# The fourth token form of the Strassen feed-forward moved to another place modulo 512 bytes in SBUF, and the softmax statistics given pools of their own

## The chip, the cores and the metric

One NeuronCore of a Trainium2 chip, one launch. The metric is the device time of the program in microseconds, the median of the runs shown. Engines are named as in the profile: PE is the matrix engine (PEld its weight loads), DVE the vector engine, ACT the scalar engine, POOL the general engine, SP the queue that issues most DMAs.

## The reference

Two decoder layers on 512 tokens of width 1024. Each layer is a SwiGLU feed-forward block, a token mixer, and a second feed-forward block, each with a residual sum and a layer norm behind it. The first layer mixes by latent attention (12 heads) and the second by three-branch sparse attention (12 heads), both with 4 heads more that attend to a memory of 256 rows. All is float32.

```python
def swiglu(x, w_gu, w_down):                 # w_gu 1024 x 5632, w_down 2816 x 1024
    g, u = jnp.split(x @ w_gu, 2, axis=-1)
    return (jax.nn.silu(g) * u) @ w_down

x = layer_norm(DN_ALPHA * x + 0.5 * swiglu(x, ffn_w_gu[layer, 0], ffn_w_down[layer, 0]), ...)
```

The four feed-forward blocks are the larger part of the time and the part that the change is about.

## The kernel before, in words

**Operands in two parts.** Every float32 operand is split into a rounded high part and the rest (`split`, L198 on ACT and L199 on DVE), and a product is three matmuls: high times high, high times low, low times high. Weights come in units of 128 x 1024 float32 by DMA (`load`), and `prep` splits each into the tiles `whi` and `wlo`, which lie in two rings (`wring`, 3 buffers, and `W.extra`, 4 buffers). `unit` and `ahead` prepare units up to four ahead of the matmuls.

**A feed-forward block** (`ffn`) has 22 slices of 128 hidden features, in five groups of 4 or 5 (`GROUPS`). Per group it first computes the hidden features and then multiplies them with the down weights (`by_units`, `prod`, L404 to L409: 512 columns a matmul). A slice is computed in one of two ways. An "s" slice is a plain product (`single`, `feature_major`, L356 to L361). A "d" slice (`seven`) is Strassen's scheme: seven products of quarter size in place of eight. Only the first group of a block has "s" slices, two or three of them; all other 77 slices are sevens.

**A seven** makes seven calls of `quarter`, each of 12 matmuls that accumulate 256 columns into half a PSUM bank: four each at L369 and L370 (weights `whi`, moving operand high and low in turn), then four at L373 (weights `wlo`, moving operand high). In order, the moving operands are a quarter of the activations (`F.xhi`, `F.xlo`), another quarter, then token form 4, form 1, form 2, form 3, and a last quarter of the activations. The forms (`F.t`, tiles `t1h` to `t4l`) are sums and differences of quarters of the activations; `token_forms` makes them once per block or takes those of the block before.

```python
            ks = slice(off + k * P, off + (k + 1) * P)
            nc.tensor.matmul(ps, lhsT=hi[:, ks], rhs=xh[:, k], start=k == 0, stop=False)
            nc.tensor.matmul(ps, lhsT=hi[:, ks], rhs=xl[:, k], start=False, stop=False)
```

**Where things lie.** Pools are laid one behind the other from the left end of SBUF, `small` and the pools of a stage from the right. Nearly all tiles are multiples of 512 bytes, so a small tile at the head of a pool sets where all that follows lies modulo 512. In the built program `wraw`, `whi`, `wlo`, the hidden features `hhi` and `hlo`, and the tiles of both attention stages lie at 256 modulo 512. The tile "offset" of 448 bytes at the head of the pool `xp` puts the activations `xhi` and `xlo`, and the pool `fm` with all token forms behind them, at 192: 64 bytes below the weights. The memory operands `mhi` and `mlo` are put at 320, 64 bytes above. The small statistics of the softmax heads (negated maximum `nm`, reciprocal sum `rs`, three buffers each) are taken from `small` by `stat`.

**What sets the order.** Nothing is scheduled by a planner: each engine runs its instructions in the order written, with semaphore waits that the framework derives from tiles, and waits on what lay before at the same addresses.

Of the kernel before, what the change touches and what calls it, by code (L numbers as in the profile page):

```python
# [9 lines left out]
F32 = mybir.dt.float32  # L10
# [7 lines left out]
P = 128  # L18
T = 512
D = 1024  # L20
NT = 4
# [82 lines left out]
def tile_trunk(ctx: ExitStack, tc, a: dict, out):  # L104
# [6 lines left out]
    small = ctx.enter_context(tc.tile_pool(name="small", bufs=1, side="right", reuse_waits="tile"))  # L111
# [123 lines left out]
        i %= 8  # L235
        return (PS.left if i < 5 else PS.right).tile([P, 512], F32, tag=f"b{i}", name="bank")

    small.tile([P, 88], F32, name="rest")

    def stat(tag, bufs):  # L240

        return small.tile([P, 2, 4], F32, tag=tag, name=tag, bufs=bufs)

    def stile():
        return PS.left.tile([P, 512], F32, tag="s", name="s", bufs=3)
# [4 lines left out]
    def s2tile():  # L250
        return PS.left.tile([P, 1024], F32, tag="s2", name="s2", bufs=2)

    def s1tile():
        return PS.left.tile([P, 512], F32, tag="s1", name="s1")
# [7 lines left out]
    def open_f(scope):  # L262
        F.st = ExitStack()
        W.extra = F.st.enter_context(tc.tile_pool(name=f"wx{scope}", bufs=NEXTRA, reuse_waits="tile"))
        F.xp = F.st.enter_context(tc.tile_pool(name=f"xp{scope}", bufs=1, reuse_waits="tile"))
        F.xp.tile([P, 112], F32, name="offset")
        F.sm = F.st.enter_context(tc.tile_pool(name=f"sm{scope}", bufs=2, reuse_waits="tile"))
        F.x = [F.xp.tile([P, D], F32, name=f"x{t}") for t in range(NT)]
        F.bk = 0
        W.scope = scope  # L270
        W.count = 0
        F.fst = ExitStack()
        F.fm = F.fst.enter_context(tc.tile_pool(name=f"fm{scope}", bufs=1, reuse_waits="tile"))

    def close_f():
        F.st.close()
        W.scope = None
        W.extra = None
        W.early = 0

    def right_pool(name, bufs=1):
        st = ExitStack()
        pool = st.enter_context(tc.tile_pool(name=name, bufs=bufs, side="right", reuse_waits="tile"))
        return st, pool
# [58 lines left out]
    def mm3(ps, ahi, alo, bhi, blo, first, last):  # L343
        nc.tensor.matmul(ps, lhsT=ahi, rhs=bhi, start=first, stop=False)
        nc.tensor.matmul(ps, lhsT=ahi, rhs=blo, start=False, stop=False)
        nc.tensor.matmul(ps, lhsT=alo, rhs=bhi, start=False, stop=last)  # L346
# [431 lines left out]

    def mla_heads(cT):
        st = ExitStack()  # L780
        hp = st.enter_context(tc.tile_pool(name="mh", bufs=1, reuse_waits="tile"))
        F.pt = hp
        va = hp.tile([P, NT, 768], F32, name="va")
# [59 lines left out]
            yield  # L843

        def head(u):
            nm, rs = stat("nm", 3)[:, 0, :], stat("rs", 3)[:, 0, :]
            pp = hp.tile([P, 1280], F32, tag="p", name="pp", bufs=5)
            pbuf[u] = pp
            pr, par = divmod(u, 2)
            qt = qts.pop(u)  # L850
            k = kx[par][pr % 2]
            for i in (3, 2, 1, 0):
                s = stile()
                q = slice(i * P, (i + 1) * P)
                n = (i + 1) * P
                nk = max(n, 256)
                po = pp[:, P_OFF[i]:P_OFF[i] + n]
                mm3(s[:, :nk], qt[:, 0, q], qt[:, 1, q], k[:, 0, :nk], k[:, 1, :nk], True, False)
                nc.tensor.matmul(s[:, i * P:n], lhsT=identb, rhs=maskb, start=False, stop=True)
                nc.vector.tensor_reduce(nm[:, i:i + 1], s[:, :n], axis=AX.X, op=ALU.max, negate=True)  # L860
                nc.scalar.activation(po, s[:, :n], AF.Exp, bias=nm[:, i:i + 1], accum_out=rs[:, i:i + 1])
                if i in (2, 0):
                    nc.vector.tensor_scalar(rs[:, i:i + 2], rs[:, i:i + 2], 1e-30, None, op0=ALU.max)
                    nc.vector.reciprocal(rs[:, i:i + 2], rs[:, i:i + 2])
                    for t in (i, i + 1):
                        po = pp[:, P_OFF[t]:P_OFF[t] + (t + 1) * P]
                        nc.gpsimd.tensor_tensor(po, po, rs[:, t:t + 1].to_broadcast([P, (t + 1) * P]), op=ALU.mult)
                yield
# [16 lines left out]
        def scores():  # L885
            yield from memory_scores(lambda n: stile())
            for u in range(HEADS):
                yield from head(u)
# [212 lines left out]

    def nsa_heads(gt, qf):
        st = ExitStack()
        hp = st.enter_context(tc.tile_pool(name="nh", bufs=1, reuse_waits="tile"))
        F.pt = hp
        F.qx.append([hp.tile([P, 2, T], F32R, name=f"q{e}") for e in ("e", "o")])
# [14 lines left out]
        def weigh(rs, gi):  # L1121

            nc.vector.scalar_tensor_tensor(rs, rs, 1e-30, gi, op0=ALU.max, op1=ALU.mult)
            nc.vector.reciprocal(rs, rs)

        def head(u):
            nm, rs = (stat(e, 3).rearrange("p a (b r) -> p (a b) r", r=2) for e in ("nm", "rs"))
            pp = hp.tile([P, 2560], F32, tag="p", name="pp", bufs=5)
            pbuf[u] = pp
            pr, par = divmod(u, 2)  # L1130
            h = pr + 6 * par
            qt = F.qx[pr % 2][par]
            kt = (S.ke, S.ko)[par]
            for i in (3, 2, 1, 0):
                s = s1tile() if i == 1 else s2tile()
                q = slice(i * P, (i + 1) * P)
                n = (i + 1) * P
                for c0 in range(0, 2 * n, 512):
                    c1 = min(c0 + 512, 2 * n)
                    for x in range(2):  # L1140
                        nc.tensor.matmul(s[:, c0:c1], lhsT=qt[:, x, q], rhs=kt[:, x, c0:c1],  # L1141
                                         start=x == 0, stop=x == 1 and c1 < 2 * n)
                nc.tensor.matmul(s[:, 2 * n - 256:2 * n], lhsT=identb, rhs=maskb[:, None, :].to_broadcast([P, 2, P]), start=False, stop=True)
                sv = s[:, 0:2 * n].rearrange("p (b r k) -> p r b k", r=2, k=P)
                po = pp[:, 2 * P_OFF[i]:2 * P_OFF[i] + 2 * n].rearrange("p (r b k) -> p r b k", r=2, k=P)
                nc.vector.tensor_reduce(nm[:, i], sv, axis=AX.XY, op=ALU.max, negate=True)
                for r in range(2):
                    nc.scalar.activation(po[:, r], sv[:, r], AF.Exp,
                                         bias=nm[:, i, r:r + 1], accum_out=rs[:, i, r:r + 1])
                if i in (2, 0):  # L1150
                    weigh(rs[:, i // 2 * 2:i // 2 * 2 + 2], gt[:, i // 2 * 2:i // 2 * 2 + 2, 3 * h + 1:3 * h + 3])
                    for ii in (i // 2 * 2, i // 2 * 2 + 1):
                        n = (ii + 1) * P
                        po = pp[:, 2 * P_OFF[ii]:2 * P_OFF[ii] + 2 * n].rearrange("p (r k) -> p r k", r=2)
                        nc.gpsimd.tensor_tensor(po, po, rs[:, ii, :, None].to_broadcast([P, 2, n]), op=ALU.mult)
                yield
# [24 lines left out]
        def scores():  # L1181
            for u in range(HEADS):
                yield from head(u)
# [50 lines left out]
    for side in ("left", "right"):  # L1234
        psum_pool(side, "f0")
    open_f(0)
    new_xt()
    new_blocks()
    sst, sp = right_pool("x0")
# [34 lines left out]
    for side in ("left", "right"):  # L1274
        psum_pool(side, "h0")
    mla_heads(cT)
    psum_pool("right", "f1")
    ast.close()
    shared_pool()
    open_f(1)  # L1280
    out_proj(0)
    mst.close()
# [14 lines left out]
    for side in ("left", "right"):  # L1297
        psum_pool(side, "h1")
    nsa_heads(gt, qf)
    psum_pool("right", "f2")  # L1300
    ast.close()
    S.st.close()
    open_f(2)
    out_proj(1)
    mst.close()
# [154 lines left out]
```

## Time and profile before

| what | value |
|---|---|
| median of 3 runs | 1894.77 us (1894.02 to 1897.25) |
| the profiled execution's own time | 1892.34 us |
| its span, from the first to the last instruction | 1890.1 us |
| PE busy | 1861.7 us, 98% |
| PEld busy | 1669.1 us, 88% |
| DVE busy | 1469.8 us, 78% |
| ACT busy | 869.5 us, 46% |
| granted TensorE clock, mean of the span | 0.997 |

The profile is of one execution. A matmul's row gives its start and a modelled end, and matmuls overlap: the time from one start to the next, here called the pace, is what a matmul costs in a stream, not its duration. Times in rows count from the first instruction.

### The profile page before, as it was taken

How to read it: one execution, taken by the hardware profiler on the slowest of the kernel's cores; microseconds unless marked ns; L12 is line 12 of the kernel's file. 1: busy time of each engine (PE TensorE's matmuls, PEld its weight loads, DVE VectorE, ACT ScalarE, POOL GpSimd, SP SyncE). 2: the span in 40 equal slices, each digit the busy share in tenths (PEclk: the TensorE clock that was granted, in tenths of full speed). 3: DMA queues.
4: the chain of work that ended last, by engine and by line, in shares of the span. 5: the costliest groups of instructions: out<-in, count | busy, mean ns of one | idle time of the engine just before them, and what ended most of it. 6: DMA issues, size and time to landing. Idle time of an engine off the chain costs nothing.

```text
span 1890.1 us, 31915 instructions
## 1 busy us (share of the span) xinstructions
PE 1861.7 (98%) x12776; PEld 1669.1 (88%) x12776; DVE 1469.8 (78%) x2362; ACT 869.5 (46%) x1435; POOL 164.2 (9%) x185
## 2 busy tenths in 40 slices
PE   9999999999999999999999999999999999999998
PEld 8999999886679999999999999998956689999997
DVE  7798788757658789788887987987577478887887
ACT  5344345446545335334663433444466344434432
POOL 0000000025500000000100000001255200000000
PEclk9999999999999999999999999999999999999999
DMA  6333335530133234234333323334321224323322
GB/s 237 112 112 109 115 101 153 171 106 27 64 112 133 80 101 134 79 101 146 115 128 113 123 79 101 123 110 158 107 50 28 94 82 138 107 83 112 114 82 74
DMA packets 59700, 203.85 MB, mean 108 GB/s; under 512 B 6944, under 2 KB 7216, under 8 KB 59552
## 3 DMA queue, kind: packets, MB, share of 16 engines
q1 hardware_dynamic: 57136, 194.70, 31.9%
q0 software_dynamic: 2416, 7.11, 1.3%
q8 instruction: 101, 1.65, 0.4%
q14 instruction: 47, 0.39, 0.1%
HBM read 188.16 MB, written 7.34 MB: 103 GB/s over the span
## 4 chain that ended last, share of the span: by engine, by line
PE 92%; DVE 3%; ACT 2%; POOL 1%; issue 1%; DMA 0%; SPq 0%; POOLq 0%; DVEq 0%; ACTq 0%
PE bank L369 13%; PE bank L373 13%; PE bank L370 13%; PE bank L408 4%; PE bank L405 4%; PE bank L406 4%; PE bank L404 4%; PE bank L407 4%; PE bank L409 4%; PE bank L361 3%; PE bank L358 3%; PE bank L356 3%; PE o L639 3%; PE tb L611 3%; PE s L1141 1%; PE bank L346 1%
## 5 line engine op out<-in xcount | busy, mean ns | idle before, releaser
L198 ACT CAST whi<-wraw 128x1024 fp32r<-128x1024 f32 (+3 forms) x479 | 463.5, 975 | 566.3 <-PE bank L409 249.3
L199 DVE TENSOR_TENSOR wlo<-wraw,whi 128x1024 fp32r<-128x1024 f32 (+3 forms) x479 | 536.4, 1126 | 129.4 <-ACT whi L198 126.3
L369 PE MATMUL bank<-t,whi 128*128 128x256 f32 x1232 | 303.1, 281 | 0.0
L370 PE MATMUL bank<-t,whi 128*128 128x256 f32 x1232 | 303.1, 280 | 0.0
L370 PEld LDWEIGHTS bank<-t,whi 128*128 128x128 f32 x1232 | 232.5, 189 | 0.0
L369 PEld LDWEIGHTS bank<-t,whi 128*128 128x128 f32 x1232 | 232.4, 189 | 0.0
L369 PE MATMUL bank<-xhi,whi 128*128 128x256 f32 x924 | 227.4, 281 | 0.0
L370 PE MATMUL bank<-xlo,whi 128*128 128x256 f32 x924 | 227.3, 280 | 0.0
L373 PE MATMUL bank<-t,wlo 128*128 128x256 f32 x1232 | 194.8, 281 | 0.0
L370 PEld LDWEIGHTS bank<-xlo,whi 128*128 128x128 f32 x924 | 174.4, 189 | 0.6
L369 PEld LDWEIGHTS bank<-xhi,whi 128*128 128x128 f32 x924 | 174.3, 189 | 0.6
L373 PEld LDWEIGHTS bank<-t,wlo 128*128 128x128 f32 x1232 | 167.3, 190 | 0.0
L308 DVE SCALAR_TENSOR_TENSOR x<-x,bank 128x512 f32<-128x512 f32 x176 | 112.6, 682 | 61.0 <-PE bank L408 58.0
L373 PE MATMUL bank<-xhi,wlo 128*128 128x256 f32 x924 | 146.1, 281 | 0.0
L356 PE MATMUL bank<-xhi,whi 128*128 128x256 f32 x544 | 131.3, 282 | 0.9 <-ACT xhi L198 0.9
L358 PE MATMUL bank<-xlo,whi 128*128 128x256 f32 x544 | 131.2, 282 | 0.9 <-DVE xlo L199 0.9
L407 PE MATMUL bank<-wlo,hhi 128*128 128x512 f32 x336 | 130.9, 390 | 0.0
L408 PE MATMUL bank<-whi,hlo 128*128 128x512 f32 x336 | 130.9, 390 | 0.0
L405 PE MATMUL bank<-whi,hhi 128*128 128x512 f32 x336 | 130.9, 390 | 0.0
L406 PE MATMUL bank<-wlo,hhi 128*128 128x512 f32 x336 | 130.8, 389 | 0.0
L404 PE MATMUL bank<-whi,hhi 128*128 128x512 f32 x336 | 130.8, 390 | 0.0
L409 PE MATMUL bank<-whi,hlo 128*128 128x512 f32 x336 | 130.8, 389 | 0.0
(330 smaller groups left out, 3550.6 us busy)
## 6 DMA issues: line engine op xcount, KB each, us to landing
wraw<-in_gu SPq DMA_DIRECT2D x175, 512.0 KB, 3.3
wraw<-in_dn SPq DMA_DIRECT2D x88, 512.0 KB, 3.8
wraw<-in_wo SPq DMA_DIRECT2D x16, 512.0 KB, 3.4
wraw<-in_wm SPq DMA_DIRECT2D x8, 512.0 KB, 4.3
x_dram<-x SPq DMA_DIRECT2D x8, 512.0 KB, 2.9
x<-x_dram SPq DMA_DIRECT2D x8, 512.0 KB, 4.4
wraw<-in_w SPq DMA_DIRECT2D x8, 512.0 KB, 4.2
wraw<-in_wq SPq DMA_DIRECT2D x6, 512.0 KB, 3.3
```

The lines of the kernel that those rows point to most:

```text
L198: nc.scalar.copy(hi, src)
L199: eng.tensor_tensor(lo, src, hi.bitcast(F32), op=ALU.subtract)
L356: nc.tensor.matmul(ps[:, c0:c1], lhsT=hi[:, k * P:(k + 1) * P], rhs=F.xhi[:, k, c0:c1], start=k == 0, stop=False)
L369: nc.tensor.matmul(ps, lhsT=hi[:, ks], rhs=xh[:, k], start=k == 0, stop=False)
L370: nc.tensor.matmul(ps, lhsT=hi[:, ks], rhs=xl[:, k], start=False, stop=False)
L373: nc.tensor.matmul(ps, lhsT=lo[:, ks], rhs=xh[:, k], start=False, stop=k == 3)
L404: nc.tensor.matmul(p0, lhsT=ahi, rhs=hi[:, 0:512], start=first, stop=False)
L405: nc.tensor.matmul(p1, lhsT=ahi, rhs=hi[:, 512:1024], start=first, stop=False)
L406: nc.tensor.matmul(p0, lhsT=ahi, rhs=lo[:, 0:512], start=False, stop=False)
L407: nc.tensor.matmul(p1, lhsT=ahi, rhs=lo[:, 512:1024], start=False, stop=False)
L408: nc.tensor.matmul(p0, lhsT=alo, rhs=hi[:, 0:512], start=False, stop=last)
L409: nc.tensor.matmul(p1, lhsT=alo, rhs=hi[:, 512:1024], start=False, stop=last)
```

## The change

Three edits, all of them of tiles' places.

In `open_f` the tiles of the pool `fm` are laid down in a written order, forms 1, 2, 3, then 320 bytes of nothing, then form 4. Forms 1 to 3 stay at 192 modulo 512, form 4 goes to 0: from 64 bytes below the weights to 256 bytes from them. (One block of raw activations, which ACT writes and DVE reads, shares a tile with form 4 and goes with it.)

The space comes from `small`: `nm` and `rs` leave it, for a pool `ms` in the latent attention and a pool `ns` in the sparse attention, each 512 bytes with its own 320 bytes of nothing. So the tiles of both attention stages lie 512 bytes higher, and those of the right side too; modulo 512 none of them moves.

On every engine the same instructions stand in the same order as before. Some 25 waits differ, on ACT, POOL, DVE and SP, because tiles now lie over other tiles of the stage before; PE's waits are the same.

```diff
-    small.tile([P, 88], F32, name="rest")
+    small.tile([P, 8], F32, name="rest")
...
         F.fm = F.fst.enter_context(tc.tile_pool(name=f"fm{scope}", bufs=1, reuse_waits="tile"))
+        for i in (1, 2, 3, 0, 4):
+            for e in "hl":
+                if i:
+                    F.fm.tile([P, 4, 256], F32, tag=f"t{i}{e}", name="place")
+            if not i:
+                F.fm.tile([P, 80], F32, name="offset")
...
     def mla_heads(cT):
         st = ExitStack()
+        sp = st.enter_context(tc.tile_pool(name="ms", bufs=1, reuse_waits="tile"))
+        sp.tile([P, 80], F32, name="offset")
...
         def head(u):
-            nm, rs = stat("nm", 3)[:, 0, :], stat("rs", 3)[:, 0, :]
+            nm = sp.tile([P, NT], F32, tag="nm", name="nm", bufs=3)
+            rs = sp.tile([P, NT], F32, tag="rs", name="rs", bufs=3)
...
     def nsa_heads(gt, qf):
         st = ExitStack()
+        sp = st.enter_context(tc.tile_pool(name="ns", bufs=1, reuse_waits="tile"))
+        sp.tile([P, 80], F32, name="offset")
...
         def head(u):
-            nm, rs = (stat(e, 3).rearrange("p a (b r) -> p (a b) r", r=2) for e in ("nm", "rs"))
+            nm = sp.tile([P, NT, 2], F32, tag="nm", name="nm", bufs=3)
+            rs = sp.tile([P, NT, 2], F32, tag="rs", name="rs", bufs=3)
```

## Rows read from the trace of the kernel before

**Rows 1.** The page, sections 1, 2 and 4: busy time and share of each engine; the granted clock in 40 slices of the span; the chain that ended last by engine.
```profile
PE 1861.7 (98%) x12776; PEld 1669.1 (88%) x12776; DVE 1469.8 (78%) x2362; ACT 869.5 (46%) x1435; POOL 164.2 (9%) x185
...
PEclk9999999999999999999999999999999999999999
...
PE 92%; DVE 3%; ACT 2%; POOL 1%; issue 1%; DMA 0%; SPq 0%; POOLq 0%; DVEq 0%; ACTq 0%
```

**Rows 2.** Groups of instructions by line on PE: line, engine, operation, out<-in, shape, count, busy us, mean ns of one, idle before. Three of the six groups that make up `quarter`; the other three have the same counts, 1232 with a token form and 924 with the activations.
```profile
L369 PE MATMUL bank<-t,whi 128*128 128x256 f32 x1232 | 303.1, 281 | 0.0
...
L369 PE MATMUL bank<-xhi,whi 128*128 128x256 f32 x924 | 227.4, 281 | 0.0
...
L373 PE MATMUL bank<-t,wlo 128*128 128x256 f32 x1232 | 194.8, 281 | 0.0
```

**Rows 3.** The timeline of PE at the seams of two groups of the first block: start us, duration us, engine, line, operation, count. 43.49 begins the first seven of the first group, 62.53 is the first down matmul behind it. 129.32 is the first down matmul of the second group, 151.08 the first matmul of the third group's sevens, 152.49 and 153.90 begin its second and third quarter (the third is form 4), 200.54 is the first down matmul behind it.
```profile
43.49 0.28 PE L369 MATMUL bank<-xhi,whi 128*128 128x256 f32 x1
...
62.53 0.39 PE L404 MATMUL bank<-whi,hhi 128*128 128x512 f32 x1
...
129.32 0.39 PE L404 MATMUL bank<-whi,hhi 128*128 128x512 f32 x1
...
151.08 0.28 PE L369 MATMUL bank<-xhi,whi 128*128 128x256 f32 x1
...
152.49 0.28 PE L369 MATMUL bank<-xhi,whi 128*128 128x256 f32 x1
...
153.90 0.28 PE L369 MATMUL bank<-t,whi 128*128 128x256 f32 x1
...
200.54 0.39 PE L404 MATMUL bank<-whi,hhi 128*128 128x512 f32 x1
```

**Rows 4.** PE in stretches that hold sevens alone: length us, PE busy us (matmuls, with two or three that still ran at the left edge), granted clock, DMA share, GB/s. The first four are the sevens of the first group of each of the four blocks (2, 2, 3 and 2 sevens), the other three are sevens of later groups (5, 4 and 4).
```profile
43.49:62.53 19.04, 19.04 (x171) 1.00 0.59 192
601.10:620.14 19.04, 19.04 (x170) 1.00 0.51 168
986.73:1015.29 28.56, 28.56 (x254) 1.00 0.46 148
1574.99:1594.03 19.04, 19.04 (x171) 1.00 0.51 166
151.08:200.54 49.46, 49.46 (x421) 1.00 0.47 152
1042.51:1082.08 39.57, 39.57 (x337) 1.00 0.42 134
1820.57:1860.15 39.58, 39.58 (x338) 1.00 0.30 94
```

**Rows 5.** The timeline of PE behind two pieces of eight transposes (L332) each, in the product of the shared keys, with the operands at 192 and 256 modulo 512. Each start at L356 is that of the second matmul behind the transposes; there are 12 matmuls from 915.15 to 916.53. A row with x8 holds eight matmuls from the first start to the last end.
```profile
915.15 0.28 PE L356 MATMUL bank<-xhi,whi 128*128 128x256 f32 x1
...
916.53 1.07 PE L361 MATMUL bank<-xhi,wlo 128*128 128x256 f32 x8
...
922.88 0.28 PE L356 MATMUL bank<-xhi,whi 128*128 128x256 f32 x1
...
923.12 1.11 PE L361 MATMUL bank<-xhi,wlo 128*128 128x256 f32 x8
```

**Rows 6.** The timeline of PE in the product of the memory's keys and values. Up to 371.99 the moving operand is `mhi` (64 bytes above the weights), from 372.11 the two have changed places (the moving operand 64 bytes below). There are 12 matmuls from 370.75 to 372.11, and 12 from there to 373.52.
```profile
370.75 0.28 PE L344 MATMUL bank<-mhi,whi 128*128 128x256 f32 x1
...
372.11 0.28 PE L344 MATMUL bank<-whi,mhi 128*128 128x256 f32 x1
...
373.52 0.28 PE L344 MATMUL bank<-whi,mhi 128*128 128x256 f32 x1
```

**Rows 7.** The timeline of PE where the compressed keys are made: the moving operand is a weight unit at 256 modulo 512, the loaded operand `zh` (64 columns) lies at 0 and 256 in turn. There are 12 matmuls from each row to the next.
```profile
946.67 0.28 PE L344 MATMUL bank<-whi,zh 128*64 128x256 f32 x1
...
948.04 0.28 PE L344 MATMUL bank<-whi,zh 128*64 128x256 f32 x1
...
949.40 0.28 PE L344 MATMUL bank<-whi,zh 128*64 128x256 f32 x1
```

**Rows 8.** The timeline of PE at a head's scores in the latent attention, 256 columns a matmul at L346.
```profile
435.02 0.28 PE L346 MATMUL s<-ke,qt 128*128 128x256 f32 x1
435.14 0.23 PE L859 MATMUL s<-cbf 128*128 128x128 bf16 x1
```

**Rows 9.** Who waited for whom: engine, line, what it waited for, us in total, times, longest us. And all engines in the sevens of the third group but the last: length, then busy us (instructions) of PE, PEld, DVE, ACT, POOL, granted clock, DMA share, GB/s.
```profile
ACT whi L198 <- PE bank L409: 249.3, 77, 10.2
...
DVE wlo L199 <- ACT whi L198: 126.3, 109, 4.5
...
151.08:190.65 39.57, 39.57 (x337) 39.57 (x336) 37.59 (x62) 19.91 (x27) 0.00 (x0) 1.00 0.40 134
```

**Rows 10.** The instructions on the tile `ko` of the latent attention: operation, count, duration ns, first and last start us; and the time from a DMA's issue to its landing.
```profile
L344 PE MATMUL s<-ko,qt x24: 279/365/479, 438.6 to 509.9; 128*128 128x256 f32 x12, 128*128 128x512 f32 x6, 128*128 128x384 f32 x6
...
L789 SPq DMA_DIRECT2D ko<-cT x2: 594/851/1108, 410.2 to 412.6; - x2
...
DMA to landing us min/median/max: 3.0/5.9/6.5
```

## The prediction, made before the change was run

> **What bounds the kernel now.** I read the page first. PE is busy 98% of the span, and the chain that ended last runs on PE for 92% [rows 1]: what makes matmuls follow each other faster shortens the program, and little else does. The granted clock is at its upper level (2.4 GHz, the slices read 9) throughout [rows 1], so no term below is a matter of the clock. Next the groups by line on PE. The sevens issue 3 x 1232 matmuls with a token form and 3 x 924 with the activations [rows 2], 6468 in all; each of the four forms has a quarter of 3696, so form 4 has 924, twelve in each of 77 sevens. Idle before them is 0.0. The mean of 281 ns is a modelled duration, not the cost; the cost is the pace, which the timeline gives.
>
> There the reader is to see that one and the same seven runs at two paces. In the first group of the first block two sevens, 168 matmuls, take from 43.49 to 62.53: 19.04 us, 113.3 ns each. In the third group five sevens, 420 matmuls, take from 151.08 to 200.54: 49.46 us, 117.8 ns each [rows 3]. Lines, shapes, clock and places modulo 512 are the same. The stretches say that this is general [rows 4]: the sevens of each block's first group run at 113.3 (19.04 us for two, 28.56 for three), those of later groups at 117.8 (39.57 or 39.58 for four). Nine sevens are fast, 68 slow. The slow pace begins with the first matmul behind the down product (151.08 to 152.49 is 1.41 us for 12, the quick pace would be 1.36), and form 4 goes on in it [rows 3]. The down product, whose two operands lie at the same place modulo 512, is quick: 96 matmuls of 512 columns from 129.32 to 151.08 are 226.7 ns each, twice 113.3 [rows 3].
>
> So there are two states in which the stream of matmuls and the weight loads under them can be, and either keeps itself up. What changes it is a break. Behind eight transposes the stream settled in the quick pace within about 12 matmuls: 1.38 us from 915.15 to 916.53, and the eight that follow take 1.07 us; behind the next eight transposes it stayed slow, with 1.11 us for eight [rows 5]. A change of the relative place does it too: when `mhi` moved from 64 bytes above the loaded operand to 64 below with no stop, 12 matmuls took 1.36 us before it and 1.41 behind it [rows 6]. The down product, then the sevens, is such a jump as well, and it always ends slow [rows 4].
>
> **The change part by part.** *The statistics' pools.* Nothing is added or removed on any engine. The tiles move by 512 bytes, which leaves them where they were modulo 512. About 25 waits differ, none on PE. One is on the DMAs into `ko`, which now wait for another weight buffer: issued at 410.2 to 412.6, landed 6.5 us later at most, first read at 438.6 [rows 10]. Some 19 us cover it; without them PE would wait at the first odd head for what is left. The other waits are on work of the stage before that ended long ago. I count nothing, and for the range 1 us either way.
>
> *Form 4 at 256 bytes.* No instruction comes or goes. Each seven now has two jumps, from the activations (64 below the weights) to form 4 (256 away) and back to form 1 (64 below). Three things can change: the pace of form 4's own 12 matmuls, the state of the rest of the seven, and the state in which the next seven begins, since nothing within a group breaks the stream.
>
> The price of the state is 117.8 - 113.3 = 4.44 ns a matmul (49.46/420 against 19.04/168). For all 68 slow sevens, 84 matmuls each, that is 5712 x 4.44 ns = 25.4 us. Out of reach stay the two quarters ahead of the first form 4 in each of 16 later groups: 384 matmuls, 1.7 us. If the jump sets the quick state, 23.7 us are gained, or 20.0 if form 4's own 816 matmuls in those sevens stay slow. Settling costs 1.38 - 1.36 = 0.02 us a time [rows 5], at most 1.5 us over 77 sevens. I take 21 us.
>
> What form 4 itself costs at 256 bytes no row shows for a load of 128 columns. The nearest has a load of 64 columns that lies at 0 and 256 in turn, and runs at 1.37 and 1.36 us for 12 [rows 7], the quick pace. The other end is a head's scores, 0.12 us from start to start (0.125 with the rounding) [rows 8]. The 256-column stream of sevens is nearer to the first, so I take between 113.3 and 117.8; the ends are a gain of 4.44 ns and a loss of 7.2 ns on each of 924 matmuls, -4.1 to +6.7 us.
>
> *Who is late next.* A quicker PE wants its weights sooner. In the slow sevens DVE is busy 37.59 of 39.57 us [rows 9], which looks tight, but what DVE waits for there is ACT's half of the split, and ACT waits for PE to free a weight buffer, 249.3 us in 77 waits [rows 9]: the splits are ahead and held back. Over the whole span DVE is at 78% [rows 1]. A group of four sevens gets shorter by 1.5 us, far less than that lead. I count nothing.
>
> A rule of the Trainium skill speaks against the whole of this. The page "TensorE: Matmul & The Clock Gate", section "Step-by-step: what each phase is for", says that PE reads SBUF through two independent ports, one for the streaming operand and one for the weight load, so that loading the next weights takes no read bandwidth from the running matmul. By it the place of form 4 would be worth 0.0 us, against the 21 of the sum. The trace here has two paces for one stream [rows 4], which that rule does not foresee, but no row shows that a conflict of addresses makes them.
>
> **The rivals.** *The jump sets the quick state* (my forecast). For it: a break ended quick in one of two cases shown, a jump can change the state within 12 matmuls, and the slow pace has nothing to bring it back until the next down product [rows 4 to 6]. 1892.34 - 21 = 1871.3 us in the profiled execution; the median of the runs shown is 2.4 above that execution, so 1873.5. Its own range is 1869 to 1879.
>
> *The jump flips the state.* Quick becomes slow as well [rows 6], so that every second seven is quick. Of two sevens, 14 quarters, six or seven gain: 34 pairs x 6.5 x 12 x 4.44 ns = 11.8 us, and the nine quick sevens lose half of theirs, 9 x 84 / 2 x 4.44 ns = 1.7. About 10 us less: 1885.
>
> *Form 4 alone is quick, and the jump back restores the slow pace.* 816 x 4.44 ns = 3.6 us: 1891.
>
> *Nothing changes.* The two states come from something else, the waits or the order at the seams, and modulo 512 does not matter; by what was said above, the skill's rule would have it so. 1894.8.
>
> *Slower: the jump always ends slow.* That is how the jump out of the down product and that of `mhi` ended [rows 4, 6]. Then the nine quick sevens lose their pace from their first form 4 on: 756 - 96 = 660 matmuls x 4.44 ns = 2.9 us. With form 4 at the dear end another 6.7: up to 1904.4. It shows as slower from a pace of form 4 of about 118.8 ns (0.9 us more over 924). The middle is 1900.
>
> **How the numbers follow.** Forecast 0.38, flip 0.17, form 4 alone 0.07, nothing 0.20, slower 0.18. A measurement of this kernel can tell about 0.2%, 3.8 us, from no change: faster is the first two, 0.55; the same is form 4 alone, nothing and the mildest end of the last, 0.28; slower 0.17. The forecast is the likeliest and stands: 1873.5. The range leaves out the last 1 to 4 us at the quick end (about 0.03) and most of the slower case: 1869 to 1898.
>
> **What would show it.** Right: the 39.57 us of a later group's four sevens become 38.1 to 38.4, with the first two quarters still at 1.41 us and the quarters behind form 4 at 1.36; the first groups stay at 19.04; the down product stays at 226.7 ns a matmul; PE still without idle time in the sevens. Flip: the four sevens at 38.8 or so, quick and slow in turn. Nothing: 39.57 again. Slower: the first groups at 19.6 or more. The forecast is wrong if form 1 behind form 4 runs at 117.8 in the later groups, or if PE begins to wait for `whi` or `wlo`.

## The result, and the profile after

The changed kernel takes 1876.73 us, median of 4 runs, against 1896.01 for the kernel before, also 4 runs: a ratio of 0.9897, 95% interval 0.988 to 0.9914, or 16 to 23 us less. Run again beside the experiments below it gave 0.9896 (0.9879 to 0.9913). The forecast was 21 us less.

The page and the groups by line on PE, after (the page's section 1; then line, engine, operation, out<-in, shape, count, busy us, mean ns of one, idle before):

```profile
PE 1844.3 (99%) x12776; PEld 1650.9 (88%) x12776; DVE 1466.2 (78%) x2362; ACT 869.8 (46%) x1435; POOL 164.2 (9%) x185
...
L375 PE MATMUL bank<-t,whi 128*128 128x256 f32 x1232 | 298.4, 278 | 0.0
```

These answer [rows 1, 2]: the same 12776 matmuls, PE busy 17.4 us less, still no idle time ahead of the sevens. The saving is therefore a matter of pace. PE in stretches of sevens alone, after (stretch; length us, PE busy us with its matmuls, granted clock, DMA share, GB/s): the first groups of the first and the third block, then three later groups.

```profile
41.34:60.55 19.21, 19.21 (x171) 1.00 0.55 190
...
975.86:1004.66 28.80, 28.80 (x255) 1.00 0.44 147
...
148.05:196.17 48.12, 48.12 (x421) 1.00 0.48 155
1031.87:1070.39 38.52, 38.52 (x337) 1.00 0.41 137
1803.68:1842.20 38.52, 38.52 (x338) 1.00 0.29 97
```

Against [rows 4], every later group is shorter (38.52 for 39.57, 48.12 for 49.46) and every first group a little longer (19.20 or 19.21 for 19.04 in three blocks, 28.80 for 28.56 in the other). All twelve groups of four read 38.51 or 38.52 and all four of five 48.12. Summed over the twenty groups the sevens take 741.1 us in place of 758.4: 17.3 us less, which is nearly all of the span's 17.9.

Where it happens shows in the timeline of PE in the third group of the first block, after (start us, duration us, engine, line, operation, count). 148.05, 149.47, 150.88, 152.31 and 153.69 begin the first five quarters of the first seven; 150.88 is form 4, 152.31 form 1, 153.69 form 2. The last three rows are from the second seven: its second quarter, its form 4 and its form 1.

```profile
148.05 0.28 PE L375 MATMUL bank<-xhi,whi 128*128 128x256 f32 x1
...
149.47 0.28 PE L375 MATMUL bank<-xhi,whi 128*128 128x256 f32 x1
...
150.88 0.28 PE L375 MATMUL bank<-t,whi 128*128 128x256 f32 x1
...
152.31 0.29 PE L375 MATMUL bank<-t,whi 128*128 128x256 f32 x1
...
153.69 0.28 PE L375 MATMUL bank<-t,whi 128*128 128x256 f32 x1
...
159.13 0.28 PE L375 MATMUL bank<-xhi,whi 128*128 128x256 f32 x1
...
160.49 0.28 PE L375 MATMUL bank<-t,whi 128*128 128x256 f32 x1
...
161.91 0.29 PE L375 MATMUL bank<-t,whi 128*128 128x256 f32 x1
```

The group starts slow as before (1.42 and 1.41 us for twelve). Form 4 takes 1.43: about 120 ns a matmul, slower than anything in the sevens before. Form 1 behind it takes 1.38, and from then on twelve take 1.36, the quick pace, through the next seven's second quarter. That seven's form 4 again costs 1.42. So a seven costs 9.60 us in place of 9.52 quick or 9.89 slow, and the first two quarters of a group keep the old price.

### The profile page after: what moved, and what is told of

Read it like the earlier page. It is cut to its first block, busy times and chain, and to the rows that moved or that the text cites. A ratio compares the mean times of both kernels' runs of the same rounds, so it can differ in the third digit from the quotient of the medians.

```text
span 1872.2 us, 31918 instructions
## 1 busy us (share of the span) xinstructions
PE 1844.3 (99%) x12776; PEld 1650.9 (88%) x12776; DVE 1466.2 (78%) x2362; ACT 869.8 (46%) x1435; POOL 164.2 (9%) x185
## 4 chain that ended last, share of the span: by engine, by line
PE 92%; DVE 3%; ACT 2%; POOL 1%; issue 1%; DMA 0%; SPq 0%; POOLq 0%; DVEq 0%; ACTq 0%
PE bank L375 13%; PE bank L379 13%; PE bank L376 13%; PE bank L411 5%; PE bank L414 5%; PE bank L412 5%; PE bank L410 5%; PE bank L413 4%; PE bank L415 4%; PE bank L367 3%; PE bank L364 3%; PE bank L362 3%; PE o L645 3%; PE tb L617 3%; PE s L1153 1%; PE bank L352 1%
## 5 line engine op out<-in xcount | busy, mean ns | idle before, releaser
L375 PE MATMUL bank<-t,whi 128*128 128x256 f32 x1232 | 298.4, 278 | 0.0
L376 PE MATMUL bank<-t,whi 128*128 128x256 f32 x1232 | 297.9, 278 | 0.0
L376 PE MATMUL bank<-xlo,whi 128*128 128x256 f32 x924 | 221.9, 277 | 0.0
L375 PE MATMUL bank<-xhi,whi 128*128 128x256 f32 x924 | 221.8, 277 | 0.0
L362 PE MATMUL bank<-xhi,whi 128*128 128x256 f32 x544 | 130.1, 280 | 0.7 <-ACT xhi L198 0.7
L364 PE MATMUL bank<-xlo,whi 128*128 128x256 f32 x544 | 130.2, 280 | 0.5 <-DVE xlo L199 0.5
```

What stands on the lines that cost most here:

```text
L364: nc.tensor.matmul(ps[:, c0:c1], lhsT=hi[:, k * P:(k + 1) * P], rhs=F.xlo[:, k, c0:c1], start=False, stop=False)
```

## Theories and experiments

**Theory 1**, as it stood behind the result: what ends a slow stretch is a short stretch of matmuls at 120 ns, which form 4 makes at its new place; the way back from it ends quick. **Rivals**: the pools do it; any jump of place does it; form 4's place in the order matters; only the place itself decides.

**The pools alone.** The 320 bytes of nothing go behind form 4, so that it stays at 192 modulo 512.

```diff
-        for i in (1, 2, 3, 0, 4):
+        for i in (1, 2, 3, 4, 0):
```

> The change with form 4 laid back at 192 modulo 512 (the 320 bytes of nothing stand behind it), so the statistics' pools alone. Theory 1 (the place of form 4 does all): 1895 us, within 0.2% of the kernel before; later groups of four sevens 39.57 us, first groups 19.04. Rival (the pools, the waits or the higher addresses do it): 1877 us, groups of four at 38.5.

Measured: 1895.93 us against 1896.5, ratio 0.9993 (0.9983 to 1.0004). PE in sevens (columns as above):

```profile
44.04:63.82 19.78, 19.78 (x170) 1.00 0.53 180
...
1046.20:1085.78 39.58, 39.58 (x338) 1.00 0.41 134
```

The later groups are as before. The pools are worth nothing that can be measured, and the rival falls. One thing is new: two of the four first groups, behind plain products with stops in them, ran slow here (19.78 for 19.04). Their quick pace in [rows 4] was how that execution fell, not a property of the place.

**Form 4 at other places**, in another place for each `open_f` (the first block; the second and third; the fourth).

```diff
-                F.fm.tile([P, 80], F32, name="offset")
+                F.fm.tile([P, (48, 16, 32)[scope]], F32, name="offset")
```

> The change with form 4 at other places: 128 above the weights in the first block, at the weights' own place in the second and third, 64 above in the fourth. Theory 1 (what counts is how far off 256 bytes are: form 4 runs at 120 ns there, and the way back from that pace ends quick): the three nearer places run form 4 at 113 to 118 and leave the pace as they find it, later groups of four at 39.5 or so. Rival (any jump out and back ends quick, however far): 38.1 to 38.5 us for four in all blocks. Second rival (each place has its own effect; a jump from the weights' own place ends slow as it does behind the down product): the second and third block slow from the first form 4 on, their first groups too (19.5 in place of 19.04), the others quick.

Measured: 1883.43 us in one run. A later group of the first block (form 4 at 128 above the weights), of the second (the same place), and the first and a later group of the fourth (64 above):

```profile
225.59:264.15 38.56, 38.56 (x337) 1.00 0.41 137
...
643.77:682.29 38.52, 38.52 (x337) 1.00 0.42 137
...
1566.13:1585.40 19.27, 19.27 (x171) 1.00 0.51 164
1612.61:1652.19 39.58, 39.58 (x338) 1.00 0.40 134
```

My theory was half wrong: at the weights' own place form 4 works just as at 256 bytes (38.52), and at 128 nearly so (38.56). Only 64 above leaves the later groups slow; in that block's first group the first seven began slow and went quick behind form 4 (19.27), the later groups never did. "Any jump of place" falls with that last block. So does "a jump from the same place ends slow": form 4 at the same place ends quick, the down product at the same place ends slow.

**The down product at other places**, on the kernel before, by a tile behind the hidden features.

```diff
+        hp.tile([P, {0: 64, 1: 16, 2: 112, 3: 32}[2 * l + f]], F32, name="offset")
         hst.close()
```

> The kernel before with the hidden features, which the down product loads, at other places: the moving operand is 256 from the loaded one in the first block, 64 above it in the second, 64 below it in the third (the sevens' own distance), 128 above in the fourth. Theory 1 (a jump from the same place is what ends slow): the third block has no jump, and its later groups run at 113.3 ns, 38.1 us for four; the first block's as well, behind some matmuls of settling; the second's slow, as behind the memory operand; the fourth open. About 6 us less for each quick block, less what the down product loses in it. Rival (the 512 columns, or the seam itself, make the slow pace wherever the operands lie): 39.57 for four in all blocks, and 1895 us.

Measured: 1897.45 us in one run. A later group of the first block (256 away), then all groups of the third (64 below; its first group has three sevens) and the first three of the fourth (128 above):

```profile
89.12:128.70 39.58, 39.58 (x338) 1.00 0.39 134
...
988.91:1017.48 28.57, 28.57 (x255) 1.00 0.45 149
1045.47:1085.04 39.57, 39.57 (x337) 1.00 0.41 134
1107.44:1155.06 47.62, 47.62 (x421) 1.00 0.42 134
1183.05:1222.63 39.58, 39.58 (x337) 1.00 0.42 134
1245.03:1283.13 38.10, 38.10 (x337) 1.00 0.49 154
1579.66:1599.45 19.79, 19.79 (x170) 1.00 0.49 160
1627.35:1665.44 38.09, 38.09 (x338) 1.00 0.43 139
1687.73:1737.20 49.47, 49.47 (x421) 1.00 0.39 128
```

At 256 the down product itself is unchanged (21.76 us between two groups) and the sevens behind it are slow, against what I expected; so are those of the second block (64 above). At 64 below and 128 above, its 96 matmuls take 22.40 and 22.29 us, and the groups behind are slow and quick by turns: each of these eight later groups runs at the other pace than the group before it. So the seam does not fix the pace by itself; in these two blocks the pace ahead of the down product still counts behind it. A down product at 226.7 ns for 512 columns is followed by slow sevens both at 256 and, as in the kernel before, at the same place. Both theories had this wrong: taking away the jump (64 below) did not give quick sevens throughout.

**Extra work at the seam**, on the kernel before, ahead of the first seven of each later group.

```diff
+    def kick(ps, w, kind):
...
+        n, c = ((4, 64), (12, 64), (12, 112))[kind - 1]
+        for _ in range(n):
+            nc.tensor.matmul(ps, lhsT=hi[:, 0:128], rhs=hi[:, c:c + 256], start=True, stop=True)
```

> The kernel before with extra work on PE between the down product and the first seven of each later group, its result overwritten: eight transposes, four matmuls at 256 bytes, twelve matmuls at 256 bytes, or twelve at the sevens' own distance, in turn over the sixteen groups, each kind four times. Theory 1 (the state is set by the jump back from 256 bytes, and nothing else is needed): groups behind the far matmuls run at 113.3, 38.1 us for four sevens, behind twelve surely and behind four perhaps; those behind the near ones stay at 39.57; transposes either way. Rival (only form 4 within each seven keeps it up, or a pause of any kind does it): all four kinds alike, 39.57 or 38.1. The extra work costs about 16 x 1.1 us, so 1880 to 1912 us.

Measured: 1898.39 us in one run. The four later groups of the first block, behind eight transposes, four and twelve matmuls at 256 bytes, and twelve at the sevens' own distance; then one in the second block behind eight transposes:

```profile
90.12:128.29 38.17, 38.17 (x339) 1.00 0.42 138
150.54:198.16 47.62, 47.62 (x422) 1.00 0.46 155
226.81:264.91 38.10, 38.10 (x339) 1.00 0.41 136
288.10:327.67 39.57, 39.57 (x339) 1.00 0.49 153
...
846.72:886.38 39.66, 39.66 (x339) 1.00 0.49 156
```

The far matmuls end quick in 8 of 8 groups, four as well as twelve; the near ones slow in 4 of 4; the transposes quick in 1 of 4. The sevens then keep the pace to the end of the group with form 4 at its old place. So other work in between is not enough by itself, and nothing inside the sevens is needed.

**Other forms far**, by another order of the tiles in `fm`: all four forms, form 4's low part alone, form 1 alone.

```diff
+        for i in (("0", "1h", "1l", "2h", "2l", "3h", "3l", "4h", "4l"),
+                  ("1h", "1l", "2h", "2l", "3h", "3l", "4h", "0", "4l"),
+                  ("2h", "2l", "3h", "3l", "4h", "4l", "0", "1h", "1l"))[scope]:
```

> The change with other forms 256 bytes from the weights, the rest at 64: in the first block all four forms, in the second and third only the low part of form 4 (4 of its 12 matmuls, each between two that read the high part at 64 bytes), in the fourth form 1 alone in place of form 4. Theory 1 (a stretch of matmuls at 120 ns, and the way back from it ends quick): first block 4 quarters at 1.44 us, one of settling and the rest at 1.36, so 39.4 to 39.5 for four sevens and 19.7 for the first two, no better than before; fourth block 38.5 as in the change; the low part alone either costs less than form 4 whole (38.2) or never reaches 120 ns and leaves the pace slow (39.6). Rival (form 4 is special by its place in the order, behind two quarters of activations): fourth block at 39.6.

Measured: 1881.99 us in one run. A later group of the first, the second and the fourth block:

```profile
90.73:130.21 39.48, 39.48 (x338) 1.00 0.39 134
...
648.05:686.42 38.37, 38.37 (x338) 1.00 0.41 138
...
1615.50:1654.08 38.58, 38.58 (x338) 1.00 0.42 137
```

As theory 1 had it, all forms far give back what is won (39.48): in a settled seven form 4 then takes 1.42 us and the three forms behind it 1.44 each, 120 ns a matmul. Form 1 alone does what form 4 did (38.58), so its place in the order is not special. The low part alone is cheaper (38.37) and ends quick in all groups. That speaks against theory 1's stretch: no two of these matmuls follow each other, and form 4 takes 1.42 us in a group's first seven and 1.40 in the second, so it does not reach 120 ns on the whole.

**How little is enough**: 1, 2 or 3 matmuls at 256 bytes, or 4 at the same place.

```diff
+        n, k, m = ((1, 0, 64), (2, 0, 64), (3, 0, 64), (4, 128, 128))[kind]
+        for _ in range(n):
+            nc.tensor.matmul(ps, lhsT=w[0][:, k:k + 128], rhs=w[0][:, m:m + 256], start=True, stop=True)
```

> The kernel before with 1, 2 or 3 matmuls at 256 bytes, or 4 matmuls whose two operands lie at the same place modulo 512, ahead of the first seven of each later group, results overwritten, each kind in four of the sixteen groups. Theory 1 (it is the stretch at 120 ns that counts; it is reached at the third matmul): 3 end quick, 38.1 us for four; 1 leaves it at 39.57; 2 either way; the 4 at the same place quick too, as form 4 was there (38.52), though the down product at the same place, at 226.7 ns, ends slow. Rival (the place itself decides): 1, 2 and 3 alike quick, and the 4 at the same place slow, as behind the down product. Extra work 16 x 0.12 to 0.48 us; in all 1875 to 1895.

Measured: 1877.95 us in one run. The four later groups of the first block, behind 1, 2, 3 and the 4:

```profile
88.91:128.49 39.58, 39.58 (x339) 1.00 0.41 134
150.53:198.14 47.61, 47.61 (x422) 1.00 0.48 157
225.71:263.81 38.10, 38.10 (x338) 1.00 0.42 139
286.06:324.16 38.10, 38.10 (x339) 1.00 0.51 160
```

One ends slow in 4 of 4 groups, two and three quick in 8 of 8, the four at the same place quick in 4 of 4. So it is not the place alone: 256-column matmuls at the same place end quick and the 512-column ones there end slow. These matmuls differ from the down product in more than width; the last experiment below keeps the down product and changes the width.

**Every distance.** 24 matmuls at the seam, at sixteen distances between the loaded and the moving operand.

```diff
+        for _ in range(24):
+            nc.tensor.matmul(ps, lhsT=w[0][:, 0:128], rhs=w[0][:, 128 + 8 * i:384 + 8 * i],
+                             start=True, stop=True)
```

> The kernel before with 24 matmuls (128 columns loaded, 256 moved, both from one weight tile, result overwritten) ahead of the first seven of each later group; the moving operand lies 0, 32, 64, ... 480 bytes modulo 512 from the loaded one, another distance in each of the sixteen groups. Theory 1: around 0 and around 256 a pace of 120 ns and a quick group of sevens behind; at 64 and 448 (the memory operand's and the sevens' distance) 117.8 and slow behind, since what comes before is the down product; at 128 near 120 and quick. Rival (only exact 0 and 256 differ): all others 117.8 and slow. Extra work 16 x 24 x 0.12 = 46 us, less 1.5 for each quick group.

Measured: 1928.55 us in one run. Stretches of the 24 matmuls at distances 0, 64 and 128, then at 256, 320 and 384 (the table has all sixteen):

```profile
91.01:93.89 2.88, 2.88 (x26) 1.00 0.50 182
...
233.28:236.10 2.82, 2.82 (x25) 1.00 0.52 186
...
658.71:661.60 2.89, 2.89 (x25) 1.00 0.55 187
...
1061.80:1064.68 2.88, 2.88 (x26) 1.00 0.56 188
...
1204.06:1206.90 2.84, 2.84 (x26) 1.00 0.49 177
...
1650.81:1653.69 2.88, 2.88 (x26) 1.00 0.53 182
```

| distance, bytes | us for 24 | sevens behind |
|---|---|---|
| 0 and 256 | 2.88, 2.88 | quick, quick |
| 32 and 288 | 2.82, 2.80 | slow, slow |
| 64 and 320 | 2.82, 2.84 | slow, slow |
| 96 and 352 | 2.89, 2.88 | slow, slow |
| 128 and 384 | 2.89, 2.88 | quick, quick |
| 160 and 416 | 2.86, 2.86 | quick, quick |
| 192 and 448 | 2.83, 2.82 | slow, slow |
| 224 and 480 | 2.84, 2.84 | quick, quick |

The rival falls. What theory 1 missed is that everything repeats after 256 bytes, the pace within 0.02 us and the end alike, in all eight pairs: by these runs "256 bytes modulo 512 from the weights" cannot be told from the weights' own place. Each distance was tried once, though, and the two of a pair stood ahead of the same group of their blocks. For 0 and 256 other runs agree at other groups (form 4, the down product, the few matmuls above); for the other pairs the repeat rests on this one run. Nor does a pace of 120 ns by itself decide: 96 bytes is as dear as 0 and ends slow, 224 is no dearer than 64 and ends quick.

**How much of it is the weight load.** The same 24 matmuls with 32, 64, 96 and 128 loaded columns.

```diff
+            nc.tensor.matmul(ps[0:n], lhsT=w[0][:, 0:n], rhs=w[0][:, 128 + d:384 + d], start=True, stop=True)
```

> The kernel before with 24 matmuls of 256 columns (both operands from one weight tile, result overwritten) ahead of the first seven of each later group. The four groups of a block load 32, 64, 96 and 128 columns in turn; the four blocks lay the moving operand 0, 64, 128 and 192 bytes modulo 512 from the loaded one. Theory 1 (what costs is the weight load under the running matmul, at places that clash): with 32 columns loaded about the quick pace of 113 ns at every distance, and the difference between distances grows with the columns, to 120, 117.8, 120 and 117.8 at 128. Rival (the place of the moving operand acts by itself, the load has no part in it, as two ports that do not disturb each other would have it): 120, 117.8, 120, 117.8 for any number of columns.

Measured: 1924.65 us in one run. The four column counts in order, at distance 0 and then at 128:

```profile
87.34:90.16 2.82, 2.82 (x25) 1.00 0.56 186
150.10:152.83 2.73, 2.73 (x26) 1.00 0.61 194
229.55:232.34 2.79, 2.79 (x26) 1.00 0.59 186
292.20:295.08 2.88, 2.88 (x25) 1.00 0.54 182
...
1057.21:1059.94 2.73, 2.73 (x25) 1.00 0.57 194
1121.30:1124.09 2.79, 2.79 (x25) 1.00 0.58 186
1200.77:1203.63 2.86, 2.86 (x26) 1.00 0.55 176
1263.50:1266.38 2.88, 2.88 (x26) 1.00 0.56 181
```

All sixteen, us for 24 matmuls and the sevens behind:

| distance, bytes | 32 columns | 64 | 96 | 128 |
|---|---|---|---|---|
| 0 | 2.82, quick | 2.73, slow | 2.79, quick | 2.88, quick |
| 64 | 2.79, slow | 2.80, quick | 2.73, slow | 2.83, slow |
| 128 | 2.73, slow | 2.79, slow | 2.86, quick | 2.88, quick |
| 192 | 2.73, quick | 2.84, quick | 2.81, quick | 2.83, slow |

The pace runs from 114 ns (2.73) to 120 (2.88) with the number of loaded columns, the moving operand unchanged. The counts stood ahead of different groups of a block, but the group is not the cause: ahead of the same group of the first block, at distance 0, 128 columns took 2.88 in the run with every distance and 32 take 2.82 here. So the load, or the narrower result that goes with it, takes part, and the rival falls. The column of 128 agrees with the table above at all four distances. My own reading is borne out at 128 bytes alone: at 0 and 64, 32 columns do not run at the quick pace, and the pace does not grow evenly with the columns. The end changes with them too (at distance 0, 64 columns end slow).

**A version without the price.** Form 4 stays where it was, and the last two down matmuls ahead of sevens, 512 columns at the same place, are issued as four of 256.

```diff
+        if halve:
+            for c in range(4):
+                nc.tensor.matmul(ps[c // 2][:, c % 2 * 256:c % 2 * 256 + 256], lhsT=alo,
+                                 rhs=hi[:, c * 256:c * 256 + 256], start=False, stop=last and c % 2 == 1)
+            return
```

> The kernel before, form 4 where it was, with the last two matmuls of each down product ahead of sevens (512 columns, operands at the same place modulo 512) issued as four of 256 columns. Theory 1 (a short stretch at 120 ns ahead of the jump ends it quick, be it at 256 bytes or at the same place): all later groups of sevens at 113.4 ns, 38.1 us for four and 47.6 for five; the four matmuls cost about 4 x 120 - 2 x 227 = 27 ns a group, 0.4 us in all; 12 x 1.47 + 4 x 1.85 - 0.4 = 24.6 us less than before, about 1872, some 5 us less than the change. Rival (the way from the down product always ends slow, or four do not do in a stream that was quick): 39.57 for four, 1895 us.

Measured: 1868.68 us, ratio 0.9862 (0.9843 to 0.9882). The change was run beside it, with this expectation:

> The change itself, beside the other two on the same chip. Theory 1: about 17 to 20 us less than before, as when it was first run; first groups 19.20, groups of four 38.52, of five 48.12.

It measured 1878.18 us, ratio 0.9896 (0.9879 to 0.9913). Its later groups came as expected; two of its first groups began slow and went quick behind form 4 (19.31 and 19.32). Three groups of sevens of the new version:

```profile
88.91:127.01 38.10, 38.10 (x339) 1.00 0.43 139
148.80:196.42 47.62, 47.62 (x423) 1.00 0.48 157
...
595.05:614.84 19.79, 19.79 (x170) 1.00 0.53 169
```

All sixteen later groups are quick from their first quarter on, the stretch of a down product grows from 21.76 to 21.79 us, and all sevens together take 734.1 us, 24.3 less than before. By the medians it is 28.5 us less, with an interval of 22 to 30. It beats the kernel before, with no tile moved. It beats the change too: the two intervals overlap by a little, but the sevens take 734.1 us against 741.3 in the profile of the change beside it. The first group of the second block fell slow (19.79), as such groups do at times.

## Why the prediction was right, and where it was not

**The bound** was right: the pace of PE in the sevens gave 17.3 of the span's 17.9 us, and PE never waited there.

**The pools** were rightly counted as nothing (0.9993).

**The two paces and their price** were right: they and the quick end behind form 4 are the mechanism that came. A slow matmul costs 4.44 ns more than a quick one, form 4 ends the slow pace in its first quarter, and the two quarters ahead of it in each later group stay slow: those were the terms behind 23.7 us.

**The mis-sized terms** are the price of form 4 and of settling. I took form 4 between 113.3 and 117.8 ns and settling as 1.5 us at most, some 2.7 us in all. Measured, a settled seven costs 9.60 us where a quick one costs 9.52, and 77 x 0.08 is 6.2 us: form 4 runs at up to 120 ns, and form 1 behind it pays again. 23.7 - 6.2 is 17.5, against 17.3 seen. The dear end of my bounds, 0.12 us from the attention scores [rows 8], had the right size. I preferred a row with 64 loaded columns [rows 7] because its stream looked nearer; the run with other column counts shows, at distance 0, 64 columns at the quick pace (2.73 us for 24) where 128 run at 120 ns (2.88). For the same reason two of my signs failed: the later groups came to 38.52 and not to 38.1 to 38.4, and the first groups did not stay at 19.04. (A slip besides: 1871.3 + 2.4 is 1873.7, not 1873.5.)

**The reason was wrong in its words, and the direction was in part luck.** That the jump would end quick I had from one break of two [rows 5], with the jumps of the down product and of `mhi` against it. At 64 bytes above, the same move would have left the later groups slow, and of the sixteen distances tried at the seam eight end quick; that 256 is one of them no row had shown. I wrote of a jump of relative place. What acts is a few 256-column matmuls at certain distances; the down product, at the same distance but 512 columns wide, has the opposite effect. And the place "256 away" behaves as the weights' own place does.

**The rivals.** The flip did not come: every later seven is quick from its form 1 on. It does occur elsewhere, from group to group, behind a down product at 64 below or 128 above (eight of eight). "Form 4 alone is quick" was the reverse of what happened. "Always ends slow" was the closest danger: form 4 at 64 bytes above leaves the later groups slow.

**The rule of independent ports.** The pace here changes with the distance between the two operands, from 2.80 to 2.89 us for 24 matmuls with 128 loaded columns, and moving form 4 was worth 17.3 us in the sevens. By the rule of the Trainium skill ("TensorE: Matmul & The Clock Gate", "Step-by-step: what each phase is for") that the weight load takes no read bandwidth from the running matmul, the place was to be worth 0.0 us; the measurement decides against that for this stream. By which path the two operands act on each other, read bandwidth or another, the runs do not show. I was right not to let the rule set the sum.

**What stays open.** Why two matmuls at distance 256 end quick, two paces can hold at one place, 96 bytes ends otherwise than 128, and fewer loaded columns end otherwise than 128 is not explained; the runs give the map, not the machinery. Outside the sevens the stretch from the last seven of the third block to the first of the fourth took 295.0 us in the change's profile and 293.6 in that before, but 293.5 to 296.5 in kernels without the pools, so I give that no cause.

## What to carry to other kernels

Where a stream of equal matmuls has the engine busy all the time, take its pace from start to start, stage by stage: two paces for one instruction can mean, as here, that what ran before has set something, and a handful of other matmuls at the seam may set it back. Look for them among work that is there anyway: splitting two wide matmuls cost 0.03 us a group and gained more than moving a tile. To price a place that the trace does not show, look for the row with the same weight load too; here it gave the better price than the row with the more similar stream.

## What the runs showed of the hardware

- The pace of a 256-column matmul with 128 loaded columns depends on the distance between its operands, between 2.80 and 2.89 us for 24, and repeats after 256 bytes within 0.02 us (eight pairs, each distance once). It changes with the number of loaded columns as well (2.73 to 2.88 at distance 0).
- At the sevens' distance the same stream holds either 113.3 or 117.8 ns a matmul to the end of its group, up to 47.6 us at the one and 49.47 at the other.
- Two or three 256-column matmuls at distance 256 are enough to end the slow pace, one is not (8 of 8 groups against 0 of 4); at distance 0 four were tried and end it too (4 of 4).
- Matmuls of 512 columns run at 226.7 ns at distances 0 and 256 (21.76 us for 96), and slower at 64 above (22.00), 128 above (22.29) and 64 below (22.40).
